# Four output tiles side by side at the three transitions of a two-layer hybrid trunk

## The chip, the core and the metric

One Trainium2 chip, one of its cores. The time is the device time of one launch in microseconds (us); three runs of the kernel before gave 1869.61, 1875.23 and 1879.98 us, median 1875.23. The engines: TensorE (PE, with its weight loads PEld), VectorE (DVE), ScalarE (ACT), GpSimd (POOL), and SyncE (SP), which issues the DMAs.

## What is computed

384 tokens (128 of context, 256 noisy latents) of width 1024 go through two layers, in float32. Each layer is a mixer and an MLP; around each stands a norm before and a norm behind, and the shift, scale and gate come from a product of the conditioning vector with a weight matrix `w_mod` (the modulation).

```python
def sandwich_block(x, mod, mix_fn, g, w_up, w_down):
    shift1, scale1, gate1, shift2, scale2, gate2 = jnp.split(mod, N_MOD, axis=-1)
    m, st = mix_fn(rmsnorm(x, g[0]) * (1 + scale1) + shift1)
    x = x + gate1 * rmsnorm(m, g[1])
    f = jnp.square(jax.nn.relu((rmsnorm(x, g[2]) * (1 + scale2) + shift2) @ w_up)) @ w_down
    x = x + gate2 * rmsnorm(f, g[3])
    return x, st
```

The mixer of layer 0 is SSD beside RWKV-7 (below: AB), that of layer 1 is GLA beside mLSTM (CD): an input projection, scans in both directions, an output projection.

## The kernel before

The residual x lies transposed as eight tiles `xT[k]` of 128 channels x 384 tokens. A dense product makes one output tile of 128 channels at a time: for each of the eight k, three matmuls, since input and weight are each split into a high and a low part (hH, hL and wH, wL): hH by wH, hL by wH, hH by wL. Weights come by DMA as float32 panels (`raw`); a copy on ScalarE makes wH and a subtraction on VectorE wL (`panel_split`). `Dense.take` asks for a panel and for as many of the next as `ahead` says; `follow` chains the dense products, so that the next one's panels are fetched while this one runs.

The run is a sequence: AB mixer, MLP 0, CD mixer, MLP 1. Between two of them lies a transition, three in all: T1 (AB to MLP 0, about 868 to 899 us in the trace), T2 (MLP 0 to CD, about 1153 to 1205 us) and T3 (CD to MLP 1, about 1585 to 1618 us). Each has these steps:

- `residual_end`: matmuls with a constant matrix (`ms`) sum the squares of the sub-layer's output m, and two more sums, into PSUM. Then come `warm` matmuls, whose result nobody reads, as many as the table `WARM` gives, and on ScalarE Ln and Exp make `rr`, the reciprocal root.
- `update(k)`, for each k: m = m * rr, then xT = xT + m. For k of `POOL_K` = (2, 5, 7) both run on GpSimd (`owner`), for the others on VectorE.
- `prescale` (into an MLP) or `prenorm` (into CD) makes hH and hL of each k. In CD the new norm's root r (`rstd`: tiles t and sx on VectorE, Ln and Exp on ScalarE) is needed first; in the MLPs r is applied to the up-product's result.
- Then the dense products begin: in an MLP the first two of 32 up tiles with their matmuls alternating (`zip`), then one by one; in CD the two of `cd_setup` (gd, the GLA gates' low rank input, and the mLSTM gates) alternating, then query, key and so on of head 0.

Before T1 and T2 a block of eight modulation steps (`mod_block`: four matmuls each, weights by DMA; `mod_end` makes `modv` and `moda` of the sum) is run off: at T1 one step in each of eight turns of the loop in `ab_out_last`, at T2 all of them after the warm matmuls. Instructions run on each engine in the order in which they are emitted; what stands behind a waiting instruction waits too.

The stage behind T2 runs the scans of eight heads (GLA and mLSTM in turn) interleaved with the dense products of the next ones.

Of the kernel before, what the change touches and what calls it, by code (L numbers as in the profile page):

```python
# [20 lines left out]
KD = 8  # L21
# [18 lines left out]
WARM = (4, 3, 0, 3, 0)  # L40
# [95 lines left out]
class Dense:  # L136


    def __init__(self, net, panels, steps):
        self.net = net  # L140
        self.cfg = net.wcfg
        self.panels = panels
        self.steps = steps
        self.w = []
        self.next = None

# [3 lines left out]
    def take(self, i):  # L150

        dn, j = self, i
        for _ in range(1 + self.cfg["ahead"]):
# [4 lines left out]
            if j == len(dn.w):  # L158
                dn.w.append(self.net.panel(dn.cfg, *dn.panels[j]))
            j += 1  # L160
        return self.w[i]


class Net:
# [258 lines left out]
    def mod_block(self, l, runs, wid, acc, sb, ahead=2):  # L423
# [9 lines left out]
        for k in range(KD):  # L433
# [4 lines left out]
            if k == KD - 1:  # L438
                self.modsb = sb()
                self.acopy(self.modsb[:, 0:wid], a)  # L440
                self.mod_end(l, runs, wid)
# [70 lines left out]
    def prenorm(self, l, pool, r, update=None, ks=range(KD)):  # L512

        out = []
        for k in ks:
            if update is not None:
                update(k)
# [24 lines left out]
    def prescale(self, l, pool, update):  # L544
# [13 lines left out]
        for k, (h, lo) in enumerate(out):  # L558
            update(k)
            coef = [(slice(a, b), self.moda[l][:, 2, k, s:s + 1]) for s, (a, b) in enumerate(SEG)]  # L560
            if k in POOL_K:
                u = self.mpool.tile([128, T], F32, tag="nh", name="nh", bufs=2)
                for q, sc in coef:
                    self.act(u[:, q], self.xT[k][:, q], AF.Copy, scale=sc)
                self.acopy(h[:, :T], u)
                self.tt(lo[:, :T], u, h[:, :T].bitcast(F32), ALU.subtract, eng=self.nc.gpsimd)
                continue
            for q, sc in coef:
                self.act(h[:, q], self.xT[k][:, q], AF.Copy, scale=sc)
            for q, sc in coef:  # L570
                self.stt(lo[:, q], self.xT[k][:, q], sc, h[:, q].bitcast(F32), ALU.mult, ALU.subtract)
        return out

    def owner(self, k):

        return self.nc.gpsimd if k in POOL_K else self.nc.vector
# [43 lines left out]
    def residual_end(self, st, ms, sx, close=None, warm=0):  # L620
# [4 lines left out]
        P = []  # L625
        for ps, a, t in zip((self.psp, self.psi, self.psp), acc, st["last"]):
# [3 lines left out]
            P.append(p)  # L630
        if st["p"] is not None:
            P.append(st["p"])
        self.warm(warm, st["last"][-1])
        r = self.mpool.tile([128, T], F32, tag="rr", name="rr", bufs=1)
        self.act(r, P[0], AF.Ln, bias=self.eps)
        self.act(r, r, AF.Exp, scale=-0.5)
# [19 lines left out]
    def panel(self, cfg, W, k0, nk, c0, ncol, placed=None):  # L656

        return self.panel_split(cfg, self.panel_raw(cfg, W, k0, nk, c0, ncol, placed))

# [37 lines left out]
    def dense_cm(self, W, c0, xs, evac, placed=None, blocks=None, ncol=128, width=T, acc=None):  # L697
# [28 lines left out]
        return Dense(self, [(W, k0, n, c0, ncol, placed) for k0, n in blocks], steps)  # L726

# [48 lines left out]
    def mlp_open(self, l):  # L776
# [31 lines left out]
        m["ups"] = [self.dense_cm(up, 128 * j, hs, lambda ps, j=j: evac_up(ps, j), width=T + 2) for j in range(32)]  # L808
# [5 lines left out]
        m["ups"][0].take(0)  # L814

    def mlp(self, before):
# [4 lines left out]
        m["hs"][:] = self.prescale(l, m["hp"], update)  # L821
        m["r"] = rstd()
        close()
# [1670 lines left out]
```

## Time and profile before

| | us |
|---|---|
| median of three runs | 1875.23 |
| profiled execution | 1876.76 |
| its span, first to last instruction | 1874.9 |
| TensorE busy in it | 1775.9 |
| VectorE busy | 1314.0 |
| ScalarE busy | 1064.5 |
| GpSimd busy | 251.0 |

The busy time of an engine is not its share of the end: an engine counts where the chain of waits goes through it. TensorE's granted clock has a mean of 0.973 of its full speed in this execution; at 1.00 it is 2.4 GHz, at 0.50 it is 1.2 GHz. Matmuls overlap, so that one lasts longer than the distance from it to the next.

### The profile page before, as it was taken

What the parts mean: (1) busy time and instruction counts of PE and PEld (TensorE: products, weight loads), DVE (VectorE), ACT (ScalarE), POOL (GpSimd) and SP (SyncE); (2) the same over time, 40 slices, a digit from 0 to 9 for tenths busy, and PEclk for the clock granted to TensorE, in tenths of its full rate; (3) what the DMA queues carried; (4) which work ended last, traced back from release to release, by engine and by line L of the source; (5) the groups of instructions that cost most, each with busy time, mean ns of one, the idle gap of its engine ahead of it and who ended that gap; (6) DMA issues with size and microseconds to landing.
All of it is one profiled execution on the core that took longest, in us unless ns stands there. A gap on an engine that the chain in (4) does not pass through costs nothing.

```text
span 1874.9 us, 37380 instructions
## 1 busy us (share of the span) xinstructions
PE 1775.9 (95%) x13653; PEld 1486.6 (79%) x13653; DVE 1314.0 (70%) x2983; ACT 1064.5 (57%) x2671; POOL 251.0 (13%) x295
## 2 busy tenths in 40 slices
PE   7889999999999999998999999799999998999998
PEld 3677767666666777785999997699989897999887
DVE  3697788777877988758766334776886958766434
ACT  3567475746564776545555332676776765655322
POOL 2221111120112011103000002020211213100000
PEclk9889999999999999999999999899999999999999
DMA  8332443333334323344445544343333233344442
GB/s 277 112 86 76 121 137 82 103 92 113 100 109 121 96 62 90 98 131 135 128 123 177 155 122 117 84 113 95 103 93 96 74 110 105 109 125 126 147 132 82
DMA packets 320252, 213.56 MB, mean 114 GB/s; under 512 B 39648, under 2 KB 305686, under 8 KB 320068
## 3 DMA queue, kind: packets, MB, share of 16 engines
q1 hardware_dynamic: 314900, 208.35, 38.7%
q10 hardware_dynamic: 4816, 2.69, 0.5%
q8 instruction: 107, 1.75, 0.4%
q14 instruction: 77, 0.63, 0.1%
q0 software_dynamic: 352, 0.13, 0.0%
HBM read 201.32 MB, written 9.78 MB: 113 GB/s over the span
## 4 chain that ended last, share of the span: by engine, by line
PE 74%; DVE 10%; ACT 7%; issue 4%; DMA 3%; POOL 1%; SPq 1%; ACTq 0%; DVEq 0%; POOLq 0%
PE dps L209 45%; PE o L209 7%; PE ps L209 4%; PE mod L209 3%; PE aux L209 2%; PE psc L209 2%; DVE wL L223 2%; PE py L209 1%; PE pt L209 1%; DVE cacc L230 1%; PE pr L209 1%; PE pw L209 1%; ACT wH L265 1%; ACT Zb L265 1%; PE ms L209 1%
## 5 line engine op out<-in xcount | busy, mean ns | idle before, releaser
L265 ACT ACTIVATE wH<-raw 128x256 fp32r<-128x256 f32 (+1 forms) x788 | 364.0, 481 | 435.6 <-PE dps L209 322.3
L223 DVE TENSOR_TENSOR wL<-raw,wH 128x256 fp32r<-128x256 f32 (+2 forms) x769 | 397.2, 534 | 240.6 <-ACT wH L265 236.9
L265 ACT ACTIVATE Zb<-pz 64x384 f16<-64x384 f32 x160 | 77.4, 484 | 36.3 <-PE pz L209 34.0
L230 DVE SCALAR_TENSOR_TENSOR cacc<-rows,params,cacc 128x192 f32<-128x192 f32 (+1 forms) x192 | 93.5, 488 | 0.7
L209 PE MATMUL dps<-sH,wH 128*128 128x384 f32 x232 | 85.6, 371 | 0.7 <-ACT sH L265 0.3
L209 PE MATMUL dps<-sH,wL 128*128 128x384 f32 x232 | 79.8, 345 | 4.4 <-DVE wL L223 4.3
L209 PE MATMUL dps<-sL,wH 128*128 128x384 f32 x232 | 80.1, 346 | 0.3 <-DVE sL L223 0.2
L209 PE MATMUL dps<-h0H,wH 128*128 128x384 f32 (+2 forms) x150 | 59.8, 403 | 14.5 <-ACT h0H L233 9.0
L223 DVE TENSOR_TENSOR AO<-AHb,rwmask 128x768 f16<-128x768 f16 (+1 forms) x112 | 60.1, 537 | 7.7 <-PE pz L209 6.0
L223 POOL TENSOR_TENSOR BK<-BK,kkk 128x768 f32<-128x768 f32 x16 | 33.8, 2112 | 221.9 <-DVE BK L227 108.1
L209 PE MATMUL dps<-h6H,wH 128*128 128x384 f32 (+2 forms) x150 | 55.8, 374 | 3.2 <-ACT wH L265 2.7
L209 PE MATMUL mod<-xT,cond 128*32 128x384 f32 (+1 forms) x320 | 55.1, 484 | 3.9 <-DVE Q L223 2.5
L223 POOL TENSOR_TENSOR gDb<-gb 128x384 f32<-128x384 f32 x28 | 34.5, 1232 | 181.4 <-DVE gb L2160 107.8
L209 PE MATMUL dps<-h4H,wH 128*128 128x384 f32 (+2 forms) x150 | 55.8, 378 | 2.1 <-ACT h4H L233 2.1
L209 PE MATMUL dps<-h0L,wH 128*128 128x384 f32 (+2 forms) x150 | 54.3, 362 | 3.4 <-DVE h0L L230 3.4
L209 PE MATMUL dps<-h2H,wH 128*128 128x384 f32 (+2 forms) x150 | 56.9, 381 | 0.0
L209 PE MATMUL dps<-h1L,wH 128*128 128x384 f32 (+2 forms) x150 | 54.4, 362 | 0.0
L209 PE MATMUL dps<-h0H,wL 128*128 128x384 f32 (+2 forms) x150 | 53.7, 358 | 0.0
L209 PE MATMUL dps<-h1H,wH 128*128 128x384 f32 (+2 forms) x150 | 53.6, 359 | 0.0
L209 PE MATMUL dps<-h1H,wL 128*128 128x384 f32 (+2 forms) x150 | 53.3, 356 | 0.0
L209 PE MATMUL dps<-h6H,wL 128*128 128x384 f32 (+2 forms) x150 | 51.8, 345 | 1.1 <-DVE wL L223 1.1
L209 PE MATMUL dps<-h2H,wL 128*128 128x384 f32 (+2 forms) x150 | 52.2, 348 | 0.0
(1118 smaller groups left out, 5496.1 us busy)
## 6 DMA issues: line engine op xcount, KB each, us to landing
raw<-in_w_mlp_up SPq DMA_DIRECT2D x64, 512.0 KB
raw<-in_w_mlp_down SPq DMA_DIRECT2D x64, 512.0 KB
raw<-in_w_in_ab SPq DMA_DIRECT2D x204, 128.0 KB
xT<-in_w_mod SPq DMA_DIRECT2D x128, 192.0 KB
raw<-in_w_in_cd SPq DMA_DIRECT2D x192, 128.0 KB
raw<-in_w_mod SPq DMA_DIRECT2D x64, 192.0 KB
raw<-in_w_mod SPq DMA_DIRECT2D x32, 256.0 KB
raw<-in_w_out_cd SPq DMA_DIRECT2D x64, 128.0 KB
```

What stands on the lines that cost most here:

```text
L209: self.nc.tensor.matmul(out, lhsT, rhs, start=start, stop=stop)
L223: (eng or self.nc.vector).tensor_tensor(out=out, in0=a, in1=b, op=op)
L230: self.nc.vector.scalar_tensor_tensor(out=out, in0=a, scalar=s, in1=b, op0=op0, op1=op1)
L265: self.nc.scalar.activation(out=out, in_=in_, func=AF.Copy)
```

## The change

1. `dense_group`: the first four output tiles of each transition run side by side in four PSUM banks. For each k twelve matmuls are issued, eight with hH and then four with hL, as soon as that k's h is there. Its panels hold two k by 512 columns (four of 512 KB in the MLPs) in place of eight k by 128. In CD the four are gd, query and key of GLA head 0, and the mLSTM gates.
2. No GpSimd in `update`, `prescale` and the CD form `renorm`: all m, xT and hL are VectorE's; ScalarE scales into a tile nh and copies it to hH.
3. `rr`'s Ln and Exp are issued behind the first of the sums.
4. Modulation products: at T1 five of the eight steps stay in the loop, at T2 three are put behind the down tiles 2, 4 and 6 of MLP 0; the rest of each block stands behind the sums, ahead of the warm matmuls, and `mod_end` comes after the group's h tiles (`mod_rest`).
5. `WARM` goes from (4, 3, 0, 3, 0) to (4, 5, 5, 3, 0): five at T2 and T3. In MLP 1 the transposes of xT (`token_major`) come after the group.

```diff
-WARM = (4, 3, 0, 3, 0)
+WARM = (4, 5, 5, 3, 0)
...
     def mod_block(self, l, runs, wid, acc, sb, ahead=2, defer=False):
...
+                if defer:
+                    self.mod_rest = rest
+                else:
+                    rest()
...
+        def steps():
+            for k, (h, lo) in enumerate(out):
+                update(k)
+                u = self.mpool.tile([128, T], F32, tag="nh", name="nh", bufs=2)
+                for s, (a, b) in enumerate(SEG):
+                    self.act(u[:, a:b], self.xT[k][:, a:b], AF.Copy, scale=self.moda[l][:, 2, k, s:s + 1])
+                self.acopy(h[:, :T], u)
+                self.tt(lo[:, :T], u, h[:, :T].bitcast(F32), ALU.subtract)
+                yield
...
+    def renorm(self, l, pool, r, update, out):
+        for k in range(KD):
             update(k)
...
+            self.tt(t, self.xT[k], r, ALU.mult)
+            for s, (a, b) in enumerate(SEG):
+                self.act(u[:, a:b], t[:, a:b], AF.Identity, bias=self.modv[l][:, k, s:s + 1], scale=self.moda[l][:, 0, k, s:s + 1])
+            self.acopy(h, u)
+            self.tt(lo, u, h.bitcast(F32), ALU.subtract)
...
         for ps, a, t in zip((self.psp, self.psi, self.psp), acc, st["last"]):
             p = ps("ms")[:, :T]
             self.mm(p, self.c("mean"), a, stop=False)
             self.mm(p, self.c("mean"), t, start=False)
+            if not P:
+                self.act(r, p, AF.Ln, bias=self.eps)
+                self.act(r, r, AF.Exp, scale=-0.5)
             P.append(p)
+        if ahead is not None:
+            ahead.split(1)
...
+        self.drain(fill)
+        self.warm(warm, st["last"][-1], bank)
...
         def update(k):
-            self.tt(ms[k], ms[k], r, ALU.mult, eng=self.owner(k))
-            self.tt(self.xT[k], self.xT[k], ms[k], ALU.add, eng=self.owner(k))
+            self.tt(ms[k], ms[k], r, ALU.mult)
+            self.tt(self.xT[k], self.xT[k], ms[k], ALU.add)
...
+    def dense_group(self, panels, parts, xs, width):
+        def steps(dn):
+            ps = [acc()[:n, :width] for acc, n, _, _, _, _ in parts]
+            for kk in range(KD):
+                ws = []
+                for (acc, n, c0, first, step, evac), p in zip(parts, ps):
+                    h, lo = dn.take(first + kk // 2 * step)
+                    h, lo = h[:, kk % 2, c0:c0 + n], lo[:, kk % 2, c0:c0 + n]
+                    ws.append((p, h))
+                    self.mm(p, h, xs[kk][0], start=kk == 0, stop=False)
+                    self.mm(p, lo, xs[kk][0], start=False, stop=False)
+                for p, h in ws:
+                    self.mm(p, h, xs[kk][1], start=False, stop=kk == KD - 1)
+                yield
...
     def mlp(self, before):
-        m["hs"][:] = self.prescale(l, m["hp"], update)
+        m["hs"][:], pre = self.prescale(l, m["hp"], update)
+        group = iter(m["ups"][0])
+        for n in (3, 1, 1, 1):
+            self.drain(self.part(pre, 4 if n == 3 else 1))
+            self.drain(self.part(group, n))
+        self.drain(pre)
...
-        self.drain(self.zip(*map(iter, m["ups"][:2])))
-        self.drain(self.pipe(m["ups"][2:]))
+        self.drain(self.pipe(m["ups"][1:]))
...
-            self.drain(self.pipe(m["downs"]))
-            r = self.residual_end(m["st"], m["ms"], self.sx, m["m"].close, WARM[1])
-            self.drain(mod)
+            for j, dn in enumerate(m["downs"]):
+                self.drain(iter(dn))
+                if j in (2, 4, 6):
+                    next(mod)
+            r = self.residual_end(m["st"], m["ms"], self.sx, m["m"].close, WARM[1], self.psi, fill=mod)
...
     def ab_out_last(self, last, close):
-            next(self.mod_tail)
+            if j < 5:
+                next(self.mod_tail)
...
     def mixer_cd(self, before):
-        hs[:] = self.prenorm(1, hp, rstd(), update)
+        pre = self.renorm(1, hp, rstd(), update, hs)
+        g = iter(group)
+        for n in range(4):
+            self.drain(self.part(pre, 2))
+            if n == 0:
+                group.split(3)
+            self.drain(self.part(g, 2))
         close()
-        self.drain(self.pipe(setup))
+        self.mod_rest()
```

TensorE at T1, from the last rows of the sums to the first matmuls with h1 (ms: sums; mod: modulation products; dps and ps: the output tiles' PSUM banks). Before:

```order
L209 MATMUL ms<-nh,const_base 128x384
L209 MATMUL ms<-acc,const_base 128x384
L209 MATMUL ms<-nt,const_base 128x384
L209 MATMUL warm<-nt,const_base 128x384 x4
L209 MATMUL dps<-h0H,wH 128x386 x2
L209 MATMUL dps<-h0L,wH 128x386
L209 MATMUL dps<-h0H,wL 128x386
L209 MATMUL dps<-h0L,wH 128x386
L209 MATMUL dps<-h0H,wL 128x386
L209 MATMUL dps<-h1H,wH 128x386 x2
```

And now:

```order
L221 MATMUL ms<-nt,const_base 128x384
L221 MATMUL mod<-raw,cond 32x384 x11
L221 MATMUL warm<-nt,const_base 128x384 x4
L221 MATMUL dps<-h0H,wH 128x386
L221 MATMUL dps<-h0H,wL 128x386
L221 MATMUL dps<-h0H,wH 128x386
L221 MATMUL dps<-h0H,wL 128x386
L221 MATMUL dps<-h0H,wH 128x386
L221 MATMUL dps<-h0H,wL 128x386
L221 MATMUL ps<-h0H,wH 128x386
L221 MATMUL ps<-h0H,wL 128x386
L221 MATMUL dps<-h0L,wH 128x386 x3
```

Eleven modulation products have moved in between the sums and the warm matmuls, and twelve matmuls use h0, where there were six, before h1 is needed.

VectorE at T1, from the last piece of the sums' input on (m, rows and rpad: the tiles of the sub-layer's output; xT: the residual's tiles). Before:

```order
L223 TENSOR_TENSOR nt<-m,xT_12177 128x384
L223 TENSOR_TENSOR m<-m,rr 128x384 x2
L223 TENSOR_TENSOR xT_12170<-xT_12170,m 128x384
L223 TENSOR_TENSOR xT_12171<-xT_12171,m 128x384
L223 TENSOR_TENSOR m<-m,rr 128x384
L230 SCALAR_TENSOR_TENSOR h0L<-xT_12170,moda_106,h0H 128x128
L230 SCALAR_TENSOR_TENSOR h0L<-xT_12170,moda_106,h0H 128x256
```

And now:

```order
L235 TENSOR_TENSOR nt<-m,xT_12177 128x384
L235 TENSOR_TENSOR m<-m,rr 128x384 x2
L235 TENSOR_TENSOR xT_12170<-xT_12170,m 128x384
L235 TENSOR_TENSOR xT_12171<-xT_12171,m 128x384
L235 TENSOR_TENSOR m<-m,rr 128x384 x2
L235 TENSOR_TENSOR xT_12172<-xT_12172,m 128x384
L235 TENSOR_TENSOR h0L<-nh,h0H 128x384
L235 TENSOR_TENSOR xT_12173<-xT_12173,m 128x384
L235 TENSOR_TENSOR h1L<-nh,h1H 128x384
```

Two instructions more stand ahead of h0L (the second m and xT of k = 2, which was GpSimd's), and h0L is one instruction in place of two.

VectorE at T2, from the last of the sixteen m and xT to the root of the next norm (t and sx; r follows on ScalarE) and the first of what uses it. Before:

```order
L223 TENSOR_TENSOR xT_12176<-xT_12176,m_16044 128x384
L223 TENSOR_TENSOR wL<-raw,wH 128x256
L227 TENSOR_SCALAR posb<-const_seq 128x128 x2
L223 TENSOR_TENSOR modv_105<-ps,params 128x4x2 x3
L230 SCALAR_TENSOR_TENSOR moda_107<-modv_105,params 128x16
L223 TENSOR_TENSOR moda_107<-modv_105,params 128x16
L223 TENSOR_TENSOR t<-rr,ms 128x384
L230 SCALAR_TENSOR_TENSOR t<-ms,t 128x384
L223 TENSOR_TENSOR t<-t,rr 128x384
L223 TENSOR_TENSOR sx<-sx,t 128x384
```

And now:

```order
L235 TENSOR_TENSOR m_16219<-m_16219,rr 128x384
L235 TENSOR_TENSOR xT_12176<-xT_12176,m_16074 128x384
L235 TENSOR_TENSOR xT_12177<-xT_12177,m_16219 128x384
L235 TENSOR_TENSOR t<-rr,ms 128x384
L242 SCALAR_TENSOR_TENSOR t<-ms,t 128x384
L235 TENSOR_TENSOR t<-t,rr 128x384
L235 TENSOR_TENSOR sx<-sx,t 128x384
L2100 COPY mn<-mn 128x8
L2362 COPY CN<-mn 128x2
L235 TENSOR_TENSOR nt<-xT_12170,r_16360 128x384
```

The three modv rows and two moda rows, which read the modulation's sum, no longer stand ahead of t; they come after the h tiles of the group.

## Rows read from the trace of the kernel before

**Rows 1.** part 4 of the page: chain that ended last, by engine

```profile
PE 74%; DVE 10%; ACT 7%; issue 4%; DMA 3%; POOL 1%; SPq 1%; ACTq 0%; DVEq 0%; POOLq 0%
```

**Rows 2.** windows: length, busy us (count) of PE, PEld, DVE, ACT, POOL; clock, DMA share, GB/s

```profile
877.00:880.00 3.00, 1.08 (x3) 0.62 (x4) 3.00 (x4) 1.66 (x5) 2.92 (x4) 0.60 0.00 0
880.00:884.00 4.00, 4.00 (x13) 3.92 (x13) 4.00 (x10) 2.86 (x8) 1.36 (x2) 0.50 0.00 0
900.00:1150.00 250.00, 248.81 (x1418) 248.17 (x1418) 131.23 (x252) 112.50 (x232) 6.72 (x8) 1.00 0.46 136
1220.00:1300.00 80.00, 79.92 (x513) 77.65 (x514) 55.23 (x118) 55.92 (x160) 10.71 (x10) 1.00 0.41 108
1300.00:1340.00 40.00, 37.96 (x241) 35.21 (x240) 38.94 (x92) 30.64 (x93) 8.18 (x10) 1.00 0.36 93
1618.00:1860.00 242.00, 242.00 (x1216) 221.01 (x1216) 125.09 (x241) 105.02 (x209) 0.00 (x0) 1.00 0.40 124
```

**Rows 3.** chain of waits at T1: start, us, what

```profile
871.79 1.82 DVE m L223 x2
873.62 2.53 DVE xT L223 x2
...
877.42 2.22 DVE h0L L230 x2
...
890.51 11.60 PE dps L209 x63
```

**Rows 4.** timeline of VectorE at T1: start, us, instruction

```profile
882.55 0.55 DVE L223 TENSOR_TENSOR xT<-xT,rows 128x384 f32<-128x384 f32 x1
883.02 0.55 DVE L223 TENSOR_TENSOR m<-m,rr 128x384 f32<-128x384 f32 x1
```

**Rows 5.** chain of waits at T2

```profile
1153.52 4.07 PE ms L209 x12
...
1159.59 3.07 PE mod L209 x33
1162.66 4.12 DMA raw<-in_w_mod
...
1166.82 5.03 PE mod L209 x18
...
1173.89 0.47 DVE t L223
...
1177.37 2.58 DVE nh L230 x3
```

**Rows 6.** groups of instructions, T1: busy us, mean ns, idle before

```profile
L223 DVE TENSOR_TENSOR wL<-raw,wH 128x512 fp32r<-128x512 f32 x6 | 4.0, 682 | 0.0
...
L209 PE MATMUL warm<-nt,const_base 128*128 128x384 f32 x8 | 2.7, 486 | 0.0
...
L233 ACT ACTIVATE nh<-xT,moda 128x256 f32<-128x256 f32 x3 | 1.5, 494 | 0.0
```

**Rows 7.** timeline of TensorE at T1

```profile
871.71 0.49 PE L209 MATMUL warm<-nt,const_base 128*128 128x384 f32 x1
```

**Rows 8.** waits at T2: us in total, times, longest

```profile
PE dps L209 <- ACT h0H L233: 5.7, 1, 5.7
...
PE ps L220 <- DVE mc L223: 1.6, 1, 1.6
```

**Rows 9.** timeline of VectorE at T2

```profile
1156.49 1.83 DVE L223 TENSOR_TENSOR m<-m,rr 128x384 f32<-128x384 f32 x2 [1.07 <-ACT rr L233]
```

**Rows 10.** timeline of TensorE behind T2

```profile
1204.85 1.18 PE L209 MATMUL ps<-gdT,gw 16*128 16x384 f32 x2 [0.66 <-DVE mwst L227]
```

**Rows 11.** timeline of TensorE at T3

```profile
1591.46 0.81 PE L209 MATMUL ms<-nh,const_base 128*128 128x384 f32 x2
```

**Rows 12.** chain of waits at T3

```profile
1604.18 1.42 PE xt L220 x12
...
1609.96 12.10 PE dps L209 x66
```

More of the change, by code (lines that the diff above doesn't have):

```diff
@@ L143, in __init__ @@
         self.steps = steps
+        self.raws = []
         self.w = []
         self.next = None
+        self.ahead = self.cfg["ahead"]
     def __iter__(self):
@@ L152, in take @@
         dn, j = self, i
-        for _ in range(1 + self.cfg["ahead"]):
+        for _ in range(1 + self.ahead):
             while dn is not None and j == len(dn.panels):
@@ L157, in take, with fetch, split @@
                 break
-            if j == len(dn.w):
-                dn.w.append(self.net.panel(dn.cfg, *dn.panels[j]))
+            dn.split(j)
             j += 1
         return self.w[i]
+    def fetch(self, i):
+        while len(self.raws) <= i:
+            self.raws.append(self.net.panel_raw(self.cfg, *self.panels[len(self.raws)]))
+    def split(self, i):
+        self.fetch(i)
+        while len(self.w) <= i:
+            self.w.append(self.net.panel_split(self.cfg, self.raws[len(self.w)]))
 class Net:
@@ L421, in mod_steps, with mod_block @@
             yield
-    def mod_block(self, l, runs, wid, acc, sb, ahead=2):
+    def mod_block(self, l, runs, wid, acc, sb, ahead=2, defer=False):
         raw = []
@@ L618, in residual_add, with residual_end @@
         st["n"] += 1
-    def residual_end(self, st, ms, sx, close=None, warm=0):
+    def residual_end(self, st, ms, sx, close=None, warm=0, bank=None, ahead=None, fill=()):
         acc = st["acc"]
         P = []
+        r = self.mpool.tile([128, T], F32, tag="rr", name="rr", bufs=1)
+        if ahead is not None:
+            ahead.split(0)
         for ps, a, t in zip((self.psp, self.psi, self.psp), acc, st["last"]):
@@ L629, in residual_end @@
             self.mm(p, self.c("mean"), t, start=False)
+            if not P:
+                self.act(r, p, AF.Ln, bias=self.eps)
+                self.act(r, r, AF.Exp, scale=-0.5)
             P.append(p)
+        if ahead is not None:
+            ahead.split(1)
         if st["p"] is not None:
             P.append(st["p"])
[L633 to L636, printed above, removed]
+        self.drain(fill)
+        self.warm(warm, st["last"][-1], bank)
         def rstd():
@@ L726, in dense_cm, with bank_y @@
         return Dense(self, [(W, k0, n, c0, ncol, placed) for k0, n in blocks], steps)
+    def dense_group(self, panels, parts, xs, width):
[11 more added lines that the diff above has]
+                    self.mm(p, h, xs[kk][1], start=False, stop=kk == KD - 1)
+                yield
+            for (_, _, _, _, _, evac), p in zip(parts, ps):
+                more = evac(p)
+                if more is not None and next(more, self) is not self:
+                    self.late.append(more)
+            yield
+        return Dense(self, panels, steps)
+    def bank_y(self):
+        return self.psy.tile([128, 512], F32, tag="y", name="dps")
     def follow(self, items):
@@ L2004, in cd_setup @@
         W = I["w_in_cd"][0]
-        first = self.dense_cm(W, 0, hs, lambda ps: self.acopy(self.gdT, ps[0:64, :]),
-                              placed=(3072, 16, 32), ncol=64)
-        first.take(0)
         self.load_const("gla", p)
```

82 lines of the change are left out of this document (42 added, 40 removed).

## The prediction

> **What bounds the kernel now.** I read the chain of waits first. It runs through TensorE for 74% of the span, through VectorE for 10%, ScalarE for 7% [rows 1]. Then the table of windows, to see where TensorE is not the bound. In MLP 0 it is busy 248.81 of 250 us, in MLP 1 242.00 of 242, in the first 80 us of the CD stage 79.92, all at full clock [rows 2]. What a transition saves is therefore handed on through the MLPs to the end. The one stretch that speaks otherwise is 1300 to 1340 us: VectorE is busy 38.94 of 40 there [rows 2]. The price of a matmul comes from the same table: 248.81 / 1418 = 0.176 us.
>
> Last, the three transitions by themselves. At T1, rr is through when VectorE begins its first m, at 871.79. Then come two m (1.82), two xT (2.53), another m, and h0L, which ends at 879.64 [rows 3]. TensorE is busy 1.08 of 3 us from 877 to 880, and then runs four full us at clock 0.50: 13 matmuls, 0.31 us each [rows 2]. What makes VectorE slow is seen where GpSimd rests: m and xT start 0.47 us apart there [rows 4], against 0.91 to 1.27 in the pairs of the chain.
>
> **The change, transition by transition.** All sums are made against the profiled execution (1876.76 us; span 1874.9), which is 1.5 us above the median of the three runs.
>
> *T1.* Three modulation steps leave the loop ahead of the sums. 33 records of these products take 3.07 us at T2 [rows 5]; a step's four products are eight records, as the four warm matmuls are [rows 6], so it costs 0.74 us, and TensorE reaches its sums up to 2.2 us earlier. VectorE works in that loop too and may not follow, so I take 1 us: rr is through at 870.8, and the sums end at 870.7 (they end where the warm matmuls start, 871.71 [rows 7]). Eleven products behind them cost 11/4 x 0.74 = 2.0, the four warm matmuls 2.6 [rows 6]; TensorE is ready at 875.3. Before h0L stand seven VectorE instructions, where two of them are new and GpSimd's before: 8 x 0.47 = 3.8, done at 874.6. ScalarE's way to h0H is shorter: xT of k = 0 at 872.2, two scalings of at most 0.49 each [rows 6] and a copy of the same kind, 873.7. So products and warm matmuls fill the wait exactly, and TensorE goes into the group without idling and at full clock: 96 x 0.176 = 16.9, end at 892.2. Before, the third and fourth tile run from 890.51 [rows 3] for 48 x 0.176 = 8.4, to 898.9. That is 6.7; I take 6 for the short waits at panel borders. What hides the rest: VectorE has 24 instructions by 0.47, six wL by 0.68 [rows 6] and four of the t chain, 17.3 us, done at 888; the last h7L is wanted at about 891.5. If that cover of 3.5 us is gone, the group is paced by VectorE, and every us over is paid. The panel of k = 4 and 5 needs the slot of the first one, and its split stands on ScalarE ahead of h5H; TensorE frees that slot four us before it needs the new panel, while two copies and two subtractions of at most 0.68 take under 3. Bounds: 0 (all of it goes to waits) and 9 (rr 2.2 earlier, no wait).
>
> *T2.* Before, t, the start of the next root, stands on VectorE behind modv, so it waits for the eight modulation steps: those run from 1159.59 to 1171.85, with 4.12 us for a late DMA in them; t starts at 1173.89, nh at 1177.37, and TensorE waits 5.7 us for h0H [rows 5, 8]. Now: three steps behind the down tiles add 2.2 to a TensorE that is the bound there. rr, through at 1156.49 [rows 9], moves to 1158.7. VectorE does sixteen m and xT alone, 7.5, and six panel subtractions between them (at most 4.1 by the 0.68 of the larger ones, which are four of these in size or two; I take 2.1): 1168.3. From t to nh it was 3.5: 1171.8. One multiplication, two scalings and a copy on ScalarE: h0H at 1173.7, which was 1180.2 (1177.37 + 2.58 and a copy). TensorE has ended its sums by 1159.8, the twenty products by 1163.5 and five warm matmuls by 1166.8; a DMA wait like the 4.12 of before is hidden in the 7 us that follow. It idles these 7 us, and I let the clock fall as at T1: 13 matmuls in the first 4 us, then 83 x 0.176 = 14.6, end at 1192.3. ScalarE, with 1.4 us per k and some 4 to 5 us of panel copies, is done near 1189. The waits on the mLSTM gate chain (1.6 and 0.66, the second seen in the row of gdT [rows 8, 10]) come back inside the value tile: 1194.6. Before, the same work, four tiles and these waits, ended at 1204.85 [rows 10]. That is 10; the modulation's end now costs TensorE something behind the group, and I take 9. Bounds: 2 (ScalarE holds the group up by one more us per k) and 12 (the clock stays up: 13 x 0.13 more).
>
> *T3.* The sums end at 1591.46 + 0.65 = 1592.1 [rows 11], unchanged. Five warm matmuls by 0.65, where there were none: 1595.4; h0L is at the latest 3.8 us behind the sums, 1595.9. The group ends at 1612.6. The 24 transposes of xT, which ran between, now follow at 1.42 / 12 = 0.118 each [rows 12]: 1615.4. Before: 1609.96 [rows 12] + 8.4 = 1618.4. Gain 3; bounds -2 and 6.
>
> Sum: 6 + 9 + 3 = 18, thus 1858.8 against the profiled execution and 1857.2 against the median. I say 1858.
>
> The row that speaks against the group is 880 to 884 us: after less than two us of idling TensorE does its work at half speed though it is fully busy [rows 2]. On this the Trainium skill, "TensorE: Matmul & The Clock Gate", section "HAM oscillation", says that a loop that waits for each next slice of k falls back to the low clock each time, and advises doing all k of one tile in a row. By that rule the change takes the wrong order. The trace agrees so far that the clock falls; whether it falls in a group that waits only briefly, no run before shows.
>
> **The rivals.** *Half clock in the groups* (the slower side): TensorE waits a little for every k, and the granted clock stays at 0.50 through the 96 matmuls. For it: T1's 880 to 884. Against it: full clock came back there by itself, in two tiles that also waited for each k. Price: 96 x 0.31 = 29.8 per group. T1 would end at 905.1 (6.2 later than before), T3 at 1595.4 + 29.8 + 2.8 = 1628.0 (9.6 later), T2 at 1173.7 + 29.8 + 2.3 = 1205.8 (1 later): 1876.8 + 17 = 1894. It decides from the second k on: if the second twelve matmuls of a group still start 0.31 apart.
>
> *T2's gain is given back in the CD stage.* GLA head 0's gate products and its scan have moved into the next stage, and VectorE is full from 1300 to 1340 [rows 2]. If that stretch sets the pace and does not start earlier, 9 are lost: 1868. Against it: its own inputs come earlier as well, and from 1220 to 1300 VectorE has 25 us free.
>
> *VectorE and ScalarE pace the groups.* With GpSimd's share on VectorE each k may take 2.5 us in place of 2.1, and panel copies in ScalarE's queue hold up the next hH: 3 us per group, 1867; if T2 is paced at 3 per k, another 6: 1873.
>
> **How the numbers follow.** A change of 0.5% (9 us here) is about what can be told from none. The forecast case (gains of 13 to 23, so 1853 to 1864) has 0.57. T2's gain given back 0.17, engines pacing the groups 0.11, half clock 0.08, and 0.07 for more than I count (under 1853). Faster by over 0.5% (under 1866): the forecast's 0.57, the 0.07, and a third of the two middle rivals, 0.09: 0.73, which I lower to 0.70, since the bounds of each term reach far. Slower: the half clock, and some 0.03 of a CD stage that reacts worse than counted: 0.11. Same: 0.19. The range runs from 1847 to 1877, past both middle rivals; the likeliest case alone has 1853 to 1864.
>
> **What would show it.** Right: at T1 and T3 TensorE goes from the warm matmuls into the first group at clock 1.00 and ends it 17 us on; at T2 nh starts near 1172 and the group ends near 1192; the CD stage then runs 8 to 10 us early up to its end. Wrong: window rows with a clock below 0.9 inside a group; waits of the group's matmuls on h tiles or wL at more than one us per k; a CD stage that ends at the old time although it began earlier.

## The result, and the profile after

The changed kernel's median is 1856.48 us (1854.43 to 1857.66, four runs), that of the kernel before, run beside it, 1876.43 (1869.61 to 1879.98). The ratio is 0.9897, interval 0.9878 to 0.9915: faster by 1.0% (16 to 23 us by the interval; 20 by the medians), where 18 us were forecast. Its profiled execution took 1855.77 us, span 1853.7.

From the page of the changed kernel, the busy times and the chain that ended last:

```profile
PE 1763.3 (95%) x13667; PEld 1479.4 (80%) x13667; DVE 1302.7 (70%) x2992; ACT 1068.7 (58%) x2688; POOL 216.8 (12%) x270
PE 76%; DVE 10%; ACT 8%; issue 3%; DMA 2%; POOL 1%; SPq 1%; DVEq 0%; ACTq 0%; POOLq 0%
```

TensorE's share of the chain rose from 74% [rows 1] to 76, and its busy time is 12.6 us less, though the two kernels have nearly as many matmuls (13653 and 13667 records): at half clock they stand 0.31 us apart [rows 2], and fewer of them now run at it. The same table of windows as [rows 2], at the places of the new kernel:

```profile
866.00:869.00 3.00, 3.00 (x12) 1.70 (x10) 3.00 (x8) 2.94 (x9) 0.00 (x0) 1.00 0.00 0
869.00:887.00 18.00, 17.74 (x103) 17.43 (x102) 13.35 (x31) 11.60 (x26) 0.00 (x0) 1.00 0.30 85
...
1152.00:1163.00 11.00, 3.93 (x15) 1.95 (x11) 9.32 (x24) 2.65 (x6) 1.01 (x6) 0.87 0.34 75
1163.00:1167.00 4.00, 3.68 (x12) 3.50 (x13) 3.21 (x7) 3.94 (x10) 0.00 (x0) 0.50 0.00 0
1167.00:1183.00 16.00, 16.00 (x93) 14.64 (x92) 7.81 (x20) 10.25 (x29) 0.52 (x2) 1.00 0.35 87
1183.00:1197.00 14.00, 12.20 (x90) 11.06 (x91) 12.74 (x37) 9.15 (x25) 0.00 (x0) 1.00 0.27 68
1220.00:1300.00 80.00, 77.00 (x495) 72.21 (x493) 60.70 (x140) 57.43 (x169) 13.28 (x15) 1.00 0.37 100
1577.00:1595.00 18.00, 18.00 (x104) 17.66 (x103) 12.82 (x27) 12.48 (x28) 0.00 (x0) 1.00 0.27 78
```

T1's gap and its half speed are gone: TensorE is busy from 866 to 887, but for 0.3 us, at clock 1.00. At T2 it still idles some 7 us and its clock is 0.50 in the four us that follow, then 1.00 through the rest of the group. From 1220 to 1300 it has three us of idling that it did not have before, 2.2 of them in the wait for gE shown below.

T1 in the chain of waits. What was m, xT, h0L and a long row of dps [rows 3] is now one run of TensorE:

```profile
860.74 3.50 PE ms L221 x12
864.24 2.07 PE mod L221 x22
866.31 2.78 PE warm L221 x8
869.09 1.05 PE dps L221 x6
```

Beside it VectorE (timeline: start, us, instruction), to be held against the 1.82 for two m and 2.53 for two xT of [rows 3]:

```profile
864.16 1.03 DVE L235 TENSOR_TENSOR m<-m,rr 128x384 f32<-128x384 f32 x2 [1.16 <-ACT rr L245]
865.10 1.02 DVE L235 TENSOR_TENSOR xT<-xT,m 128x384 f32<-128x384 f32 x2
...
867.45 0.55 DVE L235 TENSOR_TENSOR h0L<-nh,h0H 128x384 fp32r<-128x384 f32 x1
```

Each pair takes 1.02, so one starts 0.47 after the other. T2 in the chain of waits, from the root of the new norm to the first matmuls of the group, and the end of the gate chain behind it:

```profile
1157.42 0.47 DVE t L235
...
1162.38 0.48 ACT nh L245
1163.32 1.54 PE dps L221 x4
...
1194.88 0.53 ACT mem L245
1195.46 0.52 PE ps L232 x5
```

The waits from 1140 to 1230 us (us in total, times, longest):

```profile
PE dps L221 <- ACT h0H L277: 7.3, 1, 7.3
...
PE ps L221 <- DVE gE L235: 2.2, 1, 2.2
```

One wait for h0H stands where 5.7 stood [rows 8] behind modulation steps that had themselves waited. T3 in the chain of waits:

```profile
1567.35 7.00 PE ms L221 x12
1574.36 3.23 PE warm L221 x10
1577.58 1.07 PE dps L221 x6
```

**Where the time went.** The table gives distances between the starts of the same matmuls in each trace, in us. "Loop" begins with the first of the last products of the AB stage (with wlast), "downs" with MLP 0's first down matmul. "Sum" is the first matmul of a transition's sums, "T3 sums" the last of them, "4 tiles" the last of the 96 matmuls of its first four tiles, "gate" the first gate product of the second GLA head, by when all work moved at T2 has been done in any order, "5th tile" the last matmul of the fifth up tile.

```
                     before before  changed changed  no     no     t2     t own  GpSimd VectorE modv   all
                            again           again    group  warm   fill          back   only    first  three
loop ahead of T1      16.85  18.77   17.06   17.09   15.56  15.54  17.04  17.09  17.09  17.13   17.11  15.55
T1 sum -> 4 tiles     30.63  31.13   24.90   24.90   30.34  23.33  24.90  24.90  29.09  31.21   24.90  23.34
MLP 0 downs -> sum   134.98 137.57  138.52  137.67  137.56 138.22 135.97 137.13 137.97 133.77  137.62 137.78
T2 sum -> first h0    26.92  27.15   18.63   18.64   17.57  18.64  23.14  14.82  20.78  26.54   19.30  14.97
T2 h0 -> 4 tiles      23.57  24.40   18.77   18.81   23.93  19.38  19.14  18.76  19.56  26.46   18.86  17.23
T2 4 tiles -> gate    96.73  96.41   99.70   99.72   95.44 101.31 101.25 101.27  99.74  93.56   99.71  99.77
T2 sum -> gate       147.22 147.96  137.10  137.17  136.94 139.33 143.52 134.86 140.08 146.55  137.88 131.96
gate -> T3 sum       284.78 285.13  285.56  285.37  284.75 285.46 285.77 285.47 285.66 284.72  285.32 285.69
T3's twelve sums       6.42   6.61    6.52    5.63    6.43   3.93   5.62   3.93   6.40   6.24    5.63   6.34
T3 sums -> 5th tile   31.02  30.87   27.69   27.68   28.14  26.24  27.68  27.69  30.36  30.58   27.68  25.16
```

("All three" is the second version of the last experiment, below; in a kernel without a group the four tiles run two by two and one by one.) The profiled executions of before and changed differ by 21.0 us, but 3.9 of these lie ahead of 760 us, in a stage that no line of the change touches. The next two runs show that this is scatter, and from the second execution of the changed kernel (span 1857.5 against 1874.9) the sum is: T1 5.7, of the stretch ahead of it 1.3, T2 10.1, T3 4.1 (0.8 of it in the sums), less 2.7 among the down tiles, 0.5 behind the group of T1 and 0.6 in the CD stage. That is 17.4 of 17.4.

### The profile page after: what moved, and what is told of

Its sections match the earlier page's. It is cut to its first block, busy times and chain, and to the rows that moved or that the text cites. A ratio compares the mean times of both kernels' runs of the same rounds, so it can differ in the third digit from the quotient of the medians.

```text
span 1853.7 us, 37402 instructions
## 1 busy us (share of the span) xinstructions
PE 1763.3 (95%) x13667; PEld 1479.4 (80%) x13667; DVE 1302.7 (70%) x2992; ACT 1068.7 (58%) x2688; POOL 216.8 (12%) x270
## 4 chain that ended last, share of the span: by engine, by line
PE 76%; DVE 10%; ACT 8%; issue 3%; DMA 2%; POOL 1%; SPq 1%; DVEq 0%; ACTq 0%; POOLq 0%
PE dps L221 46%; PE o L221 7%; PE ps L221 5%; PE mod L221 3%; PE aux L221 2%; DVE wL L235 2%; PE psc L221 2%; PE py L221 1%; PE pt L221 1%; PE pr L221 1%; DVE cacc L242 1%; ACT wH L277 1%; ACT Zb L277 1%; PE pw L221 1%; PE ms L221 1%
## 5 line engine op out<-in xcount | busy, mean ns | idle before, releaser
L242 DVE SCALAR_TENSOR_TENSOR cacc<-rows,params,cacc 128x384 f32<-128x384 f32 (+1 forms) x192 | 94.2, 491 | 0.7
L221 PE MATMUL dps<-h0H,wH 128*128 128x384 f32 (+1 forms) x147 | 59.5, 406 | 11.9 <-ACT h0H L277 7.3
L221 PE MATMUL dps<-h4H,wH 128*128 128x384 f32 (+1 forms) x147 | 54.4, 375 | 2.1 <-ACT h4H L245 2.1
L221 PE MATMUL dps<-h2H,wH 128*128 128x384 f32 (+1 forms) x147 | 54.8, 374 | 0.0
L221 PE MATMUL dps<-h0H,wL 128*128 128x384 f32 (+1 forms) x147 | 51.9, 353 | 0.0
L221 PE MATMUL dps<-h1H,wH 128*128 128x384 f32 (+1 forms) x147 | 51.8, 352 | 0.0
L221 PEld LDWEIGHTS dps<-sH,wH 128*128 128x128 f32 x232 | 43.6, 189 | 10.1 <-issue 5.6
L221 PE MATMUL dps<-h0L,wH 128*128 128x384 f32 (+1 forms) x147 | 51.5, 356 | 0.0
L221 PE MATMUL dps<-h1H,wL 128*128 128x384 f32 (+1 forms) x147 | 51.0, 347 | 0.0
L221 PE MATMUL dps<-h1L,wH 128*128 128x384 f32 (+1 forms) x147 | 51.0, 353 | 0.0
```

Of the source, the lines that this page charges most:

```text
L221: self.nc.tensor.matmul(out, lhsT, rhs, start=start, stop=stop)
L242: self.nc.vector.scalar_tensor_tensor(out=out, in0=a, scalar=s, in1=b, op0=op0, op1=op1)
```

## The experiments

**Both kernels again, without an edit.** The question is whether the AB stage, ahead of T1, became faster or only scattered.

> The changed kernel, nothing edited. In the two profiles at hand the changed kernel is 7.2 us ahead already where T1's loop begins (844.4 against 851.6 us), although the AB stage is not edited; 3.9 of them at 760 us. Theory: this is scatter from one execution to the next in the AB stage, so the loop begins anywhere from 844 to 852 us here, while the distances behind it (loop to the end of the first four tiles, and so on) are the same to 0.5 us. Rival: something in the change speeds the AB stage up, and the loop begins at 844 to 845 us again. Time 1854 to 1860.

> The kernel before, nothing edited: a second profile. In the first one T1's first sum came 104.6 us after the last aux matmul of the AB stage; in five profiles of kernels with the change 101.6 to 103.3. Theory (the three modulation steps that left the loop are 2.2 us of it): 104 to 105 again, and T1's first sum to the end of the fourth tile 30.6, T2's first sum to GLA head 1's gates 147.2, T3's first sum to the end of the fifth tile 37.4, all within 0.7 us. Rival: these distances scatter by several us between executions, and the shares of the gain can't be read from single profiles.

The changed kernel ran in 1858.7 us (1854.76 to 1859.89), ratio 0.9907 (0.9890 to 0.9924); the AB stage's last aux product starts at 764.08 in its trace, as in the kernel before, and not at 760.14, as in the first trace. The kernel before, once, 1880.31. Behind T1's sums every transition repeats to within 0.8 us, save T3's sums: scatter holds for AB, and the shorter distances of the transitions are the change's. Two traces of a kernel do not show all of the scatter, though. Four of the traces below lose 1.5 us between T2's fourth tile and the gate product (101.3 in place of 99.7), and in one of the four, the one without warm matmuls at T1 and T3, T2 is not edited at all. It is the clock: behind the same wait of 2.17 us for gE it stays at 1.00 in some executions and is 0.50 for three us in others. Windows right behind that wait, of the changed kernel, the one without those warm matmuls and the one with t in its own buffer:

```profile
1226.00:1229.00 3.00, 3.00 (x19) 3.00 (x19) 3.00 (x12) 1.63 (x6) 1.42 (x2) 1.00 0.40 109
```

```profile
1228.00:1231.00 3.00, 3.00 (x11) 3.00 (x12) 2.26 (x5) 0.96 (x4) 0.86 (x1) 0.50 0.42 107
```

```profile
1229.00:1232.00 3.00, 3.00 (x11) 3.00 (x12) 2.25 (x6) 0.95 (x4) 0.85 (x1) 0.50 0.42 111
```

**Without the group.** The first tiles run again two by two, then one by one, with everything else of the change in place.

```diff
-        m["ups"] = [self.dense_group([(up, k, 2, 0, 512, None) for k in (0, 2, 4, 6)], ...
-        m["ups"] += [self.dense_cm(up, 128 * j, ...) for j in range(4, 32)]
+        m["ups"] = [self.dense_cm(up, 128 * j, ...) for j in range(32)]
...
-        group = self.dense_group([x for k in (0, 2, 4, 6) for x in ( ...
+        setup = [first, gates, query, key]    # one dense product each
```

> The group alone is undone at all three transitions: first two output tiles alternating, then the next ones, panels of 8 k by 128 as before (4 k by 64 for gd); no GpSimd, early rr, the moved modulation products and the warm matmuls stay. Theory (the group gains because TensorE has twelve matmuls, 2.1 us, for each k, where the h tiles come every 1.3 to 1.5 us): with six matmuls per k TensorE waits for h, 1.7 us at T1, 3.5 at T2, 2 at T3, and some of it at half clock: 8 to 12 us slower than the changed kernel, 1864 to 1868. Rival (the gain is that the h tiles come early, without GpSimd; the order of the tiles adds nothing): within 2 us of the changed kernel, under 1859.

1861.72 (1856.96 to 1865.98), ratio 0.9928 (0.9909 to 0.9948), its interval overlapping that of the changed kernel. The medians differ by 3.0, and scatter as much. By the distances the group is worth 5.4 at T1, 0.5 at T3 and nothing at T2. There its four tiles end 5.1 sooner, but 4.3 of this go again before the gate product, and 1.1 are paid before h0. The windows (columns as above) show where, first without the group:

```profile
1174.00:1194.00 20.00, 17.73 (x95) 14.53 (x94) 16.09 (x42) 14.39 (x37) 0.00 (x0) 1.00 0.29 80
1194.00:1222.00 28.00, 28.00 (x183) 27.05 (x183) 18.64 (x49) 18.86 (x54) 0.46 (x1) 1.00 0.51 131
```

TensorE idles 2.3 us inside the tiles and then never until 1222. With the group it idles 1.8 us right behind the tiles (12.20 of 14 us from 1183 on), where its next products wait for the mLSTM gate chain (mem), and again for gE, 2.2 us. The 8 to 12 us that were expected fell; the group is 3 to 6.

**The eight modulation steps of T2 all behind the sums.**

```diff
             for j, dn in enumerate(m["downs"]):
                 self.drain(iter(dn))
-                if j in (2, 4, 6):
-                    next(mod)
```

> Only at T2: the three modulation steps behind down tiles 2, 4 and 6 go back behind the sums, so that all eight stand there. In the changed kernel the three cost MLP 0 3.5 us (its lead falls from 12.2 to 8.7), while TensorE idles 7.3 us behind the warm matmuls. Theory: the steps are free in that idle time: 3.3 us faster than the changed kernel, 1853. Rival: the weights of the last three steps are late, because their buffers come free only now (4.1 us of waiting in the kernel before), and the warm matmuls and the first matmul with h0 are pushed back: no gain, 1856 to 1858.

1859.03 (1852.74 to 1863.61), ratio 0.9912 (0.9890 to 0.9933). The times alone show no difference, and the theory that these three steps cost more than they bring fell in the trace: the down tiles are 1.7 shorter (less than they scatter by), but h0 comes 4.5 later. (Up to the gate product it is 6.4; 1.5 of that is the clock behind gE.) TensorE is not why; it waits for h0H from 1166 on. The DMA queue is (its timeline: start, us, DMAs). In this kernel:

```profile
1146.51 0.42 SPq L696 DMA_DIRECT2D raw<-in_w_in_cd  x1
1152.03 5.87 SPq L411 DMA_DIRECT2D raw<-in_w_mod  x12
1158.05 1.52 SPq L696 DMA_DIRECT2D raw<-in_w_in_cd  x3
```

In the changed kernel:

```profile
1144.87 1.99 SPq L696 DMA_DIRECT2D raw<-in_w_in_cd  x4
```

The last modulation weights go into buffers that the first steps use. SyncE stands still for 5.1 us, until the first steps run behind the sums, then issues the twelve DMAs at 0.49 each, and only then the panels of CD. On VectorE the subtractions of these panels stand ahead of t, and wait:

```profile
1162.66 0.29 DVE L235 TENSOR_TENSOR wL<-raw,wH 128x128 fp32r<-128x128 f32 x1 [3.73 <-ACT wH L277]
...
1164.15 0.55 DVE L235 TENSOR_TENSOR t<-rr,ms 128x384 f32<-128x384 f32 x1
```

So t starts at 1164.15, 17.2 behind the first sum, where it is 12.7 in the changed kernel.

**modv ahead of t again**, as in the kernel before, all else as changed (`mod_block` without `defer`; the call of `mod_rest` behind the group goes).

```diff
-    lambda: self.mpool.tile([128, T], F32, tag="nt", name="modsb", bufs=2), 5, True)
+    lambda: self.mpool.tile([128, T], F32, tag="nt", name="modsb", bufs=2), 5)
```

> The changed kernel, except that at T2 the end of the modulation (its sum's copy, the three small matmuls, modv and moda) is done at once behind the last product, so that modv and moda stand on VectorE ahead of t again, as in the kernel before. Theory (what t waited for was the products, 12.3 us with a late DMA; they end early now): modv is ready before VectorE has got through its m and xT; T2's first sum to the first matmul with h0 is longer by modv and moda alone, 0.5 to 1 us: 19.1 to 19.6 in place of 18.6. Rival (the place in the queue is what cost): 21 us or more.

One run, 1859.49; h0 19.30 behind the sum, in place of 18.64: 0.7 us, as expected, with modv in the chain of waits but nothing ahead of it to wait for:

```profile
1158.03 0.23 DVE modv L235 x2
...
1161.84 0.46 DVE t L235
```

**No warm matmuls at T1 and T3**, five still at T2.

```diff
-WARM = (4, 5, 5, 3, 0)
+WARM = (0, 5, 0, 3, 0)
```

> No warm matmuls at T1 and T3 (the table is 0, 5, 0, 3, 0). In the changed kernel they end 1.4 us (T1) and 2.5 us (T3) after h0H is ready. Theory A (the clock is held by the group itself, and by what stands ahead of it): the groups begin that much earlier at clock 1.00: 3.5 to 4 us faster than the changed kernel, 1852 to 1853. Rival (the pause between sums or fill and the first matmul with h0 drops the clock, as the rule on the clock gate has it): a group at half clock for 4 us costs 1.8 us per place and up to 13 if it stays: 1857 to 1870, with granted clocks near 0.5 in the first 4 us of the group.

1857.79 (1853.14 to 1866.31), ratio 0.9912 (0.9888 to 0.9936): the times alone don't tell it from the changed kernel. The distances do: 1.6 less at T1, 1.4 less at T3 behind the sums, 3.0 where 3.5 to 4 were expected, each time with the group at full clock (windows of the two groups):

```profile
870.50:888.00 17.50, 17.46 (x101) 17.47 (x102) 14.30 (x32) 12.87 (x29) 0.00 (x0) 1.00 0.25 67
...
1577.40:1594.00 16.60, 16.58 (x94) 16.60 (x95) 13.93 (x28) 12.49 (x28) 0.00 (x0) 1.00 0.23 66
```

At both places it was the warm matmuls that ended last, and the group waited for them. At T3 they also read the tile that the next nh is written to: "ACT nh" waits 1.2 us for "PE warm" in the changed kernel.

**The root ahead of the updates.** t shared the buffers of nt, and in VectorE's order it stood behind all sixteen m and xT. With r2's buffer it stands behind the first three.

```diff
-            t = self.mpool.tile([128, T], F32, tag="nt", name="t", bufs=2)
+            r2 = self.mpool.tile([128, T], F32, tag="ssq", name="r2", bufs=1)
+            t = r2
```

> The changed kernel with one buffer changed: t, the first tile of the next root, is kept in r2's own buffer and no longer takes one of the two nt buffers, so that it need not wait for one. At T2 the four t and sx instructions then stand on VectorE behind the first three of the sixteen m and xT, where they stood behind all sixteen. Theory (at T2 the wait for h0H, 7.3 us of idle TensorE, is VectorE's sixteen instructions ahead of t, no longer the modulation): r comes 6 us earlier, nt of k = 0 then stands behind 12 m and xT and 6 panel pieces, and the first matmul with h0 comes 3 to 4 us earlier, 15 us after the first sum in place of 18.6; 3 to 4 us faster, 1854 to 1855. Rival (as with the group at T2, what is won is given back in the CD stage, where the mLSTM gates' chain sets the pace): the distance from T2's first sum to GLA head 1's first gate product stays at 137.2 us.

1857.52 (1850.84 to 1857.63), ratio 0.9896 (0.9867 to 0.9926). The t chain (written to r) now runs among the first updates on VectorE:

```profile
1156.02 0.55 DVE L235 TENSOR_TENSOR r<-rr,ms 128x384 f32<-128x384 f32 x1
...
1164.12 0.56 DVE L235 TENSOR_TENSOR nt<-xT,r 128x384 f32<-128x384 f32 x1
```

h0 comes 14.82 behind the sum, 3.8 sooner, as expected, and the fourth tile ends 3.9 sooner. Up to the gate product 2.3 are left in this trace; the 1.5 between are the half clock behind gE (the third of the windows above), which the kernel without those warm matmuls shows too, with T2 unedited. So it is not shown that the gate chain takes any of the root's gain back, and the distance to the gate product fell, against the rival. In the times the 3 to 4 us expected do not show.

**GpSimd back**, with k = 2, 5 and 7: their m and xT at all transitions, their hL at T1 and T3, their nt at T2; the rest as changed.

```diff
-                self.tt(lo[:, :T], u, h[:, :T].bitcast(F32), ALU.subtract)
+                self.tt(lo[:, :T], u, h[:, :T].bitcast(F32), ALU.subtract, eng=self.nc.gpsimd if k in POOL_K else None)
...
-            self.tt(t, self.xT[k], r, ALU.mult)
+            self.tt(t, self.xT[k], r, ALU.mult, eng=self.nc.gpsimd if k in POOL_K else None)
...
+            e = self.nc.gpsimd if k in POOL_K else None
-            self.tt(ms[k], ms[k], r, ALU.mult)
-            self.tt(self.xT[k], self.xT[k], ms[k], ALU.add)
+            self.tt(ms[k], ms[k], r, ALU.mult, eng=e)
+            self.tt(self.xT[k], self.xT[k], ms[k], ALU.add, eng=e)
```

> GpSimd has its share back: m, xT of k = 2, 5, 7 at all transitions, hL of these at T1 and T3, nt of these at T2. The group, the early rr, the moved products and warm matmuls stay. Theory (VectorE's m and xT take 1.3 us instead of 0.55 while GpSimd works, so h0L comes 7.9 us after rr, not 3.8): the group starts 3 to 4 us later at T1 and 1 to 2 later at T3, where the warm matmuls cover the rest, and pauses for the late k = 2; T2 as it is: 5 to 7 us slower than the changed kernel, 1862 to 1865. Rival (GpSimd's 8 us run beside VectorE, the slower VectorE is made up for by fewer instructions): within 2 us of the changed kernel.

1867.01 (1861.44 to 1876.2, ten runs), ratio 0.9959 (0.9942 to 0.9976): 8 to 12 us slower than the changed kernel, by medians and ratios, more than expected; in the traces 4.2 at T1, 2.9 at T2, 2.7 at T3. VectorE at T1:

```profile
871.78 1.83 DVE L235 TENSOR_TENSOR m<-m,rr 128x384 f32<-128x384 f32 x2 [1.16 <-ACT rr L245]
873.54 2.62 DVE L235 TENSOR_TENSOR xT<-xT,m 128x384 f32<-128x384 f32 x2
876.08 1.34 DVE L235 TENSOR_TENSOR m<-m,rr 128x384 f32<-128x384 f32 x1
```

Five instructions take 5.6 us beside GpSimd where they take 2.4 without it. In these 5.6 us GpSimd finishes four of its own, at 1.30 to 1.37 each: two engines do in that time nine instructions, VectorE alone, at 0.47 each, would do twelve. At T1 the group was expected to start 3 to 4 us later. It starts 0.8 later, since the warm matmuls cover the rest, and is 3.4 longer: TensorE has done its eight matmuls with h0H when it waits for h0L, and the twelve that follow run at half clock.

```profile
880.50 1.11 PE L221 MATMUL dps<-h0L,wH 128*128 128x386 f32 x3 [1.77 <-DVE h0L L235]
...
880.50:884.00 3.50, 3.50 (x12) 3.50 (x13) 3.50 (x7) 3.01 (x8) 1.00 (x1) 0.54 0.00 0
```

(The first is a row of TensorE's timeline, the second of the windows.)

**VectorE alone in the kernel before.**

```diff
-POOL_K = (2, 5, 7)
+POOL_K = ()
```

> The kernel before with one edit: POOL_K is empty, so that VectorE does m, xT and the h tiles of all k at the three transitions; no group, nothing moved. Theory (GpSimd's share slows VectorE from 0.55 to 1.3 us, and this delays h0L; putting it back into the changed kernel cost 4.2 us at T1, 2.9 at T2 and about 3 at T3): T1 from first sum to the fourth tile's end 3 to 4 us shorter than 30.6 to 31.1, T3 to the fifth tile's end 2 to 3 shorter than 37.4; at T2 the root waits for the modulation all the same, so 147.2 to 148.0 stays within 1: 5 to 8 us faster than the kernel before, 1867 to 1870. Rival (without the group VectorE, now with all sixteen m and xT and two-piece hL, paces the tiles): no faster than the kernel before, over 1872.

1881.3 (1873.85 to 1886.14, ten runs), ratio 1.0019 (1.0001 to 1.0038): no gain, where 5 to 8 us were expected; the rival said so. h0 does come 3.1 us sooner at T1 and 2.8 at T3, but the tiles end 0.3 to 0.4 sooner at T3 and no sooner at T1. TensorE at T1, the last matmul of the first two tiles and the next:

```profile
885.66 0.34 PE L209 MATMUL dps<-h7H,wL 128*128 128x386 f32 x1
889.36 0.66 PE L209 MATMUL dps<-h0H,wH 128*128 128x386 f32 x1 [3.37 <-DVE nt L223]
```

and VectorE meanwhile:

```profile
885.67 0.56 DVE L223 TENSOR_TENSOR sx<-sx,t 128x384 f32<-128x384 f32 x1
...
887.42 1.33 DVE L223 TENSOR_TENSOR wL<-raw,wH 128x512 fp32r<-128x512 f32 x2
888.66 1.01 DVE L223 TENSOR_TENSOR nt<-dps,r 128x384 f32<-128x384 f32 x2
```

Two tiles give TensorE 48 matmuls, which are through as soon as the last h is. Then their banks must be emptied (nt), and that stands on VectorE behind the rest of its queue: 3.4 us of wait, and the clock falls to 0.88 in the windows behind. At T3 the wait for the banks is 3.3 us; at T2 modv waits for the modulation steps whatever VectorE does, 9.3 us. So at T1 GpSimd's removal and the group pay only together: four tiles in four banks are 17 us of matmuls, in which VectorE gets through. (Without the group, T1 is at 30.34, and the wait for nt is 2.5 us there.) At T3 it is not so. The kernel without the group needs 28.14 there, 0.5 more than the changed one and 2.7 to 2.9 less than before, and its trace has no wait for nt. Its h0 begins 2.6 us later than here, behind the five warm matmuls, and the form of h and the place of the transposes are others as well; which of these spares it the wait, no run separates.

**All three: the root early, no warm matmuls at T1 and T3,** first with the five of T2 and then with eleven there, which fill TensorE's wait for h0.

```diff
-WARM = (4, 5, 5, 3, 0)
+WARM = (0, 5, 0, 3, 0)    # first, and t in r2's buffer
+WARM = (0, 11, 0, 3, 0)   # second, the same
```

> t in r2's buffer, and no warm matmuls at T1 and T3. If both gains stand (3.5 us at T2, 1.6 at T1 and 3.1 at T3, as in the run without warm matmuls), 8 us faster than the changed kernel: 1849 to 1851. If T2's gain is given back in the CD stage: 1853 to 1854.

> The best so far (t in r2's buffer, no warm matmuls at T1 and T3), and at T2 eleven warm matmuls in place of five, so that TensorE is busy until about 0.3 us before h0 is there (it idled 4 us). Theory: the group at T2 then runs at full clock from its first matmul, 17.2 us in place of 19.3, and T2's first sum to the gates of head 1 gets 1 to 2 us shorter than 135.4: 1850 to 1852 by the clock of this chip's runs. Rival (the CD stage takes it back): the group is shorter, the distance to head 1's gates is not.

The first ran in 1852.43 (1847.52 to 1858.03), ratio 0.9882 (0.9857 to 0.9906), between its two forecasts; the second in 1850.94 (1850.25 to 1852.46), ratio 0.9856 (0.9840 to 0.9872). The second is 26 us under the kernel before and some 6 to 10 under the changed one, and its interval lies below both of the changed kernel's (0.9878 to 0.9915 and 0.9890 to 0.9924). The first's overlaps all three. T2 in it:

```profile
1152.00:1162.00 10.00, 10.00 (x58) 5.01 (x50) 10.00 (x26) 2.92 (x6) 1.01 (x6) 1.00 0.40 87
...
1164.00:1180.00 16.00, 16.00 (x93) 14.43 (x91) 10.31 (x25) 12.60 (x33) 0.52 (x2) 1.00 0.36 87
```

TensorE does not idle, the clock stays at 1.00, and the four tiles take 17.23 where they took 18.8. These warm matmuls end about when h0H is there, and they pay: the fourth tile ends 1.4 sooner behind the sum than with the early root alone, and 1.9 sooner than in the first version. (Up to the gate product it is 2.9; the other 1.5 are the clock behind gE, which stayed up in this execution.) The nine of T1 and T3 did not pay.

## Why the prediction was right, step by step

*T1, 6 us, of which 1 in the loop ahead.* From the first sum to the end of four tiles the forecast's own times are 24.7 us (867.5 to 892.2); 24.90 were measured. That it comes out so close is two misses that cancel. From start to start, the sums took 2.7 us against 3.2, the eleven products 2.07 against 2.0, the warm matmuls 2.4 against 2.6, and the group 17.8 against 16.9 (96 x 0.176), at clock 1.00; the forecast had kept 0.7 aside for waits in the group. "Products and warm matmuls fill the wait exactly" was not quite so: without the warm ones the group starts 1.4 us sooner, so they overfill it. The 1 us in the loop is not shown: it lasted 16.85, 18.77 and 17.13 with eight steps, and 15.5 or 17.1 with five.

*T2, 9 us.* First sum to first group matmul: 18.1 forecast (1155.6 to 1173.7), 18.64 measured; 7 us of idling, 7.3 measured; clock 0.50 for 4 us, as said; group 18.6 against 18.8. Behind the group the sum was too high. Its 10 has the 2.2 of the three steps already taken off; counted from T2's first sum it is 12.5 (51.5 before, 39.0 after), and up to the gate product 10.1 were measured. The forecast let the waits behind the tiles grow by 1.3 and they grew by 3.0; the 2.2 us for gE are in no term of it. Net of the three steps T2 gave 7.4 in this pair, 7.9 with their mean of 2.2, where 9 were taken. The 2.2 among the down tiles fits as a mean: 137.8 over the eight traces with the three steps in the table, 135.6 over the four without them, though each kind scatters by 1.4 to 3.8. One reason was only half of it. The prediction had t wait behind modv for the eight steps. With the steps spread, modv's place ahead of t costs 0.7; what had made the root late was what modv waited for, the eight steps behind the sums and the weights that they wait for. Each put back alone into the changed kernel, the three steps cost 4.5, GpSimd 2.1, modv 0.7: 7.3 of the 8.3 between 26.92 and 18.64. "A DMA wait like the 4.12 of before is hidden" was right in its result, but by the placing of those steps and not by the 7 us of idling: with all steps behind the sums it is not hidden, because it delays the panels of CD in the same queue.

*T3, 3 us.* 3.3 behind the sums. The sums vary by themselves, with the clock (below). Taken out alone, the group costs 0.5 of them, GpSimd's removal 2.7.

*The sum.* In the pair of traces that adds up to 17.4, the terms of the forecast are worth 5.7, 7.4 and 3.3, less the 0.5 and 0.6 that went behind T1's group and in the CD stage: 15.3. The other 2.1 are the 1.3 ahead of T1 and the 0.8 in T3's sums, which vary by as much without an edit. The mechanisms held, but that the total met 18 so closely is in part luck.

*The rivals.* Half clock in the groups: only the first four us of T2's, as forecast; at T1 and T3 the second twelve matmuls start 0.18 apart. With GpSimd back, where TensorE waits 1.8 us for h0L inside T1's group, twelve of the matmuls behind do run at half clock, and then the clock is back. The rule of the Trainium skill ("TensorE: Matmul & The Clock Gate", section "HAM oscillation") against an order by slices of k speaks of loops that wait for each slice, and does not apply where the next slice is there in time: 17.77 us for 96 matmuls at clock 1.00. T2's gain given back in the CD stage: 3.0 go between the fourth tile and the gate product, 0.6 behind it, of 13.0. For one part the rival was right: the group's own 5.1 goes whole, 4.3 of it at the gate chain, within 100 us. VectorE and ScalarE pacing the groups: 17.1 to 18.8 per group say no, while in the kernel before with all of GpSimd's share on VectorE and two tiles, VectorE does pace (3.4 us at T1).

What the sum didn't know is how far its parts depend on each other: taken out of the changed kernel one by one, the group is 3 to 6, GpSimd's removal 8 to 12, the spread steps some 3 (4.5 less 1.7, in the trace alone), the place of modv 1, about the whole; put into the kernel before by itself, GpSimd's removal is nothing.

## What to carry over

Before an engine is freed of waits, look at what stands behind it in the next engine's queue: at T1 h0 came three us sooner with VectorE alone and the time stayed, until TensorE had four banks of work to do while VectorE emptied its queue. Place a step by the queue that feeds it: three steps moved ahead cost TensorE some 2 us and brought h0 4.5 sooner, because their weights no longer held up other panels. Warm matmuls are worth it where the wait is longer than they are, and cost their length past that point where it isn't. Before a distance from one trace is put down to an edit, look at the clock in its windows: 1.5 us came and went at gE, 2.7 at T3's sums, with no edit there.

## What the runs showed of the hardware

The twelve sums of T3 take 3.93 us or 5.6 to 6.6, in kernels whose code there is the same. Windows over them, of the changed kernel and of the one with t in its own buffer:

```profile
1567.40:1573.90 6.50, 6.50 (x12) 3.49 (x13) 4.87 (x12) 2.57 (x6) 0.00 (x0) 0.55 0.29 82
```

```profile
1571.80:1575.80 4.00, 3.95 (x12) 2.09 (x13) 3.43 (x9) 1.94 (x5) 0.00 (x0) 1.00 0.47 135
```

TensorE waits for VectorE in both before it (2.7 us and 3.4 us). In the changed kernel its clock had fallen to half 4 us earlier, in the other kernel it had done so some 12 us earlier and was back. So up to 2.7 us at T3 come and go with where the clock falls, and T3 is best compared from the last sum on.

GpSimd beside VectorE: a tensor-tensor of 128x384 starts 0.47 us after the one before when GpSimd rests, and beside GpSimd's, of 1.30 to 1.37 each, five of them take 5.6 us, 1.1 each. The Trainium skill ("SBUF — State Buffer", section "Who interferes with whom") says that a VectorE instruction with two inputs from SBUF contends with GpSimd's reads, and one of them waits for the other; these rows agree so far that VectorE gets slower.
